# Up projection of a two-layer decoder: late weight sums pinned to their columns, their tiles taken from other rings, put-off halves in five steps, and the next layer's parameters loaded earlier

## Chip, cores and metric

The kernel runs on one core of a Trainium2 chip. The metric is the device time of one execution in microseconds. Before the change it is 1697.03 us, the median of three runs (1696.28 to 1697.89). The engines are called PE (TensorE, matrix multiply), DVE (VectorE), ACT (ScalarE), POOL (GpSimd) and SP (SyncE). Each runs its own instructions in the order in which they stand in its row of the program; SP, POOL and ACT also issue transfers (DMA).

## What is computed

Two residual layers on 512 positions of width 1024, all in float32. Each layer has a token mixer (three branches) and then a gated MLP with a causal convolution of width 3. The change lies around the MLP:

```
def conv_ffn(h, w_up, conv_w, conv_b, w_down):
    S = h.shape[1]
    u = h @ w_up
    up = jnp.pad(u, ((0, 0), (CONV_WIDTH - 1, 0), (0, 0)))
    c = conv_b
    for j in range(CONV_WIDTH):
        c = c + conv_w[j] * up[:, j:j + S]
    gate, val = jnp.split(c, 2, axis=-1)
    return (jax.nn.silu(gate) * val) @ w_down
...
    for l in range(DEPTH):
...
        x = x + conv_ffn(rmsnorm(x, norm2_g[l]), ffn_w_up[l], ffn_conv_w[l], ffn_conv_b[l], ffn_w_down[l])
    return rmsnorm(x, final_g)
```

Here w_up is 1024 x 5632 and w_down is 2816 x 1024 for each layer.

## The kernel before

**Products in three passes.** A float32 product is made of three faster ones: each operand is split into a high part and a rest. For a weight tile of 128 x 512 (a unit), `load` (L124) brings the raw tile `wr` by an SP transfer, `part` (L164) makes the high part by a copy on ACT (L175, `sh` or `wh`) and the rest by a subtraction on DVE (L178, `sl` or `wl`), and `mm3` (L190, L194) issues the three matmuls. `unit` (L97) runs loading and splitting some units ahead of their use, by a plan that a first pass over the program has recorded.

**Up projection, `ffn_up` (L1169).** 44 columns in pairs i = 0 to 21, the gate column and then the value column. For each column `colF` makes 24 matmuls on two units. Then DVE scales the result (`fu`, L1197), ACT makes the first tap of the convolution (`cv`, L1199), and DVE the other two (L1200, L1201). After a pair comes the gated product `fth` (L1206 on ACT, L1207 on DVE). Two pairs make a piece for the down projection, which works on 2 x 2 blocks with fewer products than the plain form: `halves` (L1217) prepares sums and differences of two products `fth`, for the last piece as `hs` and `hd`. It is a generator, called on in steps; the steps of the last piece are put off into the down projection, where `tail4` (L1250) takes one at each of its calls n = 3, 4, 5 and 6. Parts of the pieces are also written to memory (`ab` and `s4`, on POOL) and loaded again later.

**Late sums, `presum` (L283).** The down projection also needs sums of four blocks of w_down. `PRE` (L27) lists which are made in the up projection: nine groups in layer 0, starting at columns 4, 8, ..., 36, and five in layer 1, at 4, 12, 20, 28 and 36. A group loads one tile `pre` in each of four columns (SP), makes one sum in each of the next four (`sum4`, L162, on DVE), and each sum is written to memory (`ts`) by POOL (`store4`, L303), one column later than its place in the code. The down projection loads it again as a weight. Groups in `NOW` (L29) are loaded and summed in the down projection of layer 1 itself (tiles `now`).

**Tiles.** Ring u has 31 tiles, ring r 16, pool f 39. A sum tile comes from f when its group starts before column 20, otherwise from u in layer 1 and from r in layer 0. Weight parts of the up projection come from these rings too; a new tile waits until the old one in its place has been read for the last time. Which place it gets is decided by the scheduler that builds the program.

**Order.** A scheduler puts the instructions of each engine into a row by priority, which is the order of the code with some parts raised. `kept` (L119) pins an instruction to its place among the pinned ones, as long as `self.keep` is set, which holds in the up projection from i = 2 on. Before the change the loads of `pre` and the splits are pinned, the sums are not.

**Parameters.** `load_pc` (L479) loads a layer's parameter columns (`pc`, 128 x 242) on ACT's queue. For layer 1 it is called at the start of `down` (L1257); five small DVE operations (`omu`, `haw`, `hka`, `oka`, `nkk`, L573 to L581) read it.

Of the kernel before, what the change touches and what calls it, by code (L numbers as in the profile page):

```python
# [53 lines left out]
class Emit:  # L54
# [228 lines left out]
    def presum(self, l, c):  # L283

        for at, q in PRE[l].items():
            n = c - at
            if 0 <= n < 4:
                self.pre[l, q, n] = t = (self.f if at < 20 else self.u if l else self.r)(n="pre")
                self.kept(self.nc.sync.dma_start(t, self.raw4(l, q, (1, 3, 0, 2)[n])))
            if 4 <= n < 8:  # L290
                b = [self.pre[l, q, k] for k in (2, 0, 3, 1)]
                p = (7, 5, 6, 4)[n - 4]
                self.stores.append(((l, q), p, self.sum4(b, p)[0]))
            if 5 <= n < 9:
                self.store4(n=1)
# [116 lines left out]
    def run(self):  # L412
# [24 lines left out]
        for step in "z0 w z1 w z2 w z3 s0 s1 w z4 s2 z5 s3 w c z6 s4 w z7 s5 s6 s7 w w".split():  # L437
            if step == "w":
                if self.plan:
                    if self.nraw == self.npart:  # L440
                        self.load(self.plan[self.nraw])
                    self.part(self.plan[self.npart])
            elif step == "c":
                g1 = self.pc
                self.load_pc(0)
                tc.keep_in_program_order(nc.scalar.dma_start(self.con, a["con"]))
                self.pc, g1 = g1, self.pc
            elif step[0] == "z":
                self.norm_z(st, xs[int(step[1])], "n1")
            else:  # L450
                self.norm_sq(st, xs[int(step[1])])
# [27 lines left out]
    def load_pc(self, l):  # L479
        self.pc = self.sp.tile([128, NPC], F32, name=self.nm("pc"), tag="pc")  # L480
        self.tc.keep_in_program_order(self.nc.scalar.dma_start(self.pc, self.a["pcols"][l]))

# [83 lines left out]
    def rwkv(self, l, nst):  # L566
# [61 lines left out]
        def prep(m):  # L628
# [25 lines left out]
            A.activation(tha, pA, AF.Tanh, scale=0.5, bias=haw[:, m:m + 1])  # L654
            V.tensor_tensor(x[:, :, 64:128], q8(r), Ein, op=MUL)
            V.scalar_tensor_tensor(x[:, :, 0:64], q8(k), self.p("kk", m), Eex, op0=MUL, op1=MUL)
            V.scalar_tensor_tensor(kkn, tha, 1.0, k, op0=ADD, op1=MUL)
            A.activation(tha, tha, AF.Identity, scale=hka[:, m:m + 1], bias=oka[:, m:m + 1])
            V.scalar_tensor_tensor(bk[:, :, 0, :], q8(kkn), nkk[:, m:m + 1], q8(Eout), op0=MUL, op1=MUL)
            kp = k  # L660
            V.tensor_tensor(kp, k, tha, op=MUL)
            V.tensor_tensor(bk[:, :, 1, :], q8(kp), q8(Eout), op=MUL)
            f = F[:, m, 0:7]
# [505 lines left out]
    def ffn_up(self, l, st, x):  # L1169
# [10 lines left out]
        for i in range(NFF):  # L1180
# [6 lines left out]
            for j in (i, NFF + i):  # L1187
# [14 lines left out]
                cs.append(t)  # L1202
                self.presum(l, 2 * i + len(cs) - 1)
            g, v = cs
            th = self.u(n="fth")
# [11 lines left out]
    def halves(self, l, a, b, q, at):  # L1217
# [4 lines left out]
        else:  # L1222
            s, d = self.u(n="hs"), self.u(n="hd")
        ab = self.dp.tile([128, 512], F32, name=self.nm("ab"))
# [11 lines left out]
        V.tensor_tensor(s[:, h[0]], a[:, h[1]], b[:, h[1]], op=ADD)  # L1236
        V.tensor_tensor(s[:, h[1]], s[:, h[0]], a[:, h[0]], op=SUB)
        V.tensor_tensor(d[:, h[0]], b[:, h[0]], s[:, h[1]], op=SUB)
        P.dma_start(self.s4[:, h[q % 2]], d[:, h[0]])
# [10 lines left out]
    def tail4(self, act, n):  # L1250

        if 2 < n < 7:
            next(self.tail, None)
# [3 lines left out]
    def down(self, act, x, st):  # L1257


        nc, V, A, P, po = self.nc, self.nc.vector, self.nc.scalar, self.nc.gpsimd, self.tc.keep_in_program_order  # L1260
        self.load_pc(1)
        Q, H, N = NFF // 2, [slice(0, 256), slice(256, 512)], {}
# [450 lines left out]
```

## Time and profile before

One execution was profiled. Its own time is 1696.14 us, its span in the trace 1694.4 us, its mean granted clock 0.998.

| | |
|---|---|
| median of three runs | 1697.03 us |
| profiled execution, its own time | 1696.14 us |
| its span | 1694.4 us |
| ACT busy | 819.1 us (48%) |
| POOL busy | 295.2 us (17%) |
| HBM read and written | 233.25 MB and 56.89 MB |

Stages, in us from the start of the span: mixer of layer 0 up to about 500, its up projection to 738, its down projection to 867, mixer of layer 1 to 1345, its up projection to 1583, its down projection (`last`) to the end.

A row of the timeline gives start, length, engine, line of the kernel, operation, and output and inputs by the program's names without numbers; in brackets stands how long the engine was idle before, and for what. A row of a group gives busy time, the mean of one instruction in ns, and the idle time of its engine just before. A row of waits gives total, number and longest.

### The profile page before, as it was taken

The numbers are of one execution on the slowest core, as the hardware profiler recorded it, in microseconds if no ns is written. First come the engines' busy times: TensorE is split into PE (matmuls) and PEld (weight loads), VectorE is DVE, ScalarE is ACT, GpSimd is POOL, SyncE is SP. The second block draws the span as 40 slices with busy tenths as digits, with TensorE's granted clock in tenths as the row PEclk, the third lists the DMA queues.
The fourth block names the chain that finished last, engine by engine and source line by source line (L and its number), as shares of the span: only waits on it lengthen the run. The fifth ranks groups of instructions, "written<-read, shape, count | busy, mean of one in ns | idle before, by whom it ended". The sixth has DMA issues, their size and how long they took to land.

```text
span 1694.4 us, 29267 instructions
## 1 busy us (share of the span) xinstructions
PE 1677.2 (99%) x10643; PEld 1393.3 (82%) x10643; DVE 1290.5 (76%) x2289; ACT 819.1 (48%) x1436; POOL 295.2 (17%) x438
## 2 busy tenths in 40 slices
PE   9999999999999999999999999999999999999998
PEld 7888877888888887789988887778888888888787
DVE  7887746578578988887868877565785688888886
ACT  6563533554254444456655634335543444444565
POOL 1121013312200111100111210223132022221000
PEclk9999999999999999999999999999999999999999
DMA  5236565634434665667733365646344445555865
GB/s 182 90 110 210 183 201 162 187 119 137 162 115 152 216 209 191 202 222 262 232 112 95 106 202 178 210 154 193 121 141 144 155 162 182 192 186 171 283 193 173
DMA packets 155904, 292.09 MB, mean 172 GB/s; under 512 B 21552, under 2 KB 32560, under 8 KB 155760
## 3 DMA queue, kind: packets, MB, share of 16 engines
q1 hardware_dynamic: 127136, 213.97, 39.9%
q0 software_dynamic: 20272, 61.10, 10.6%
q10 hardware_dynamic: 8352, 15.15, 2.5%
q8 instruction: 83, 1.36, 0.3%
q14 instruction: 61, 0.50, 0.1%
HBM read 233.25 MB, written 56.89 MB: 171 GB/s over the span
## 4 chain that ended last, share of the span: by engine, by line
PE 71%; issue 16%; DVE 5%; DMA 4%; POOL 2%; ACT 1%; SPq 0%; ACTq 0%; DVEq 0%; POOLq 0%
PE acc L194 60%; PE sm L194 5%; PE sm L766 2%; DMA pre<-wdt 2%; DMA wr<-wall 1%; PE sm L1022 1%; DVE sl L178 1%; POOL ts L303 1%; PE sm L673 1%; DVE wl L178 1%; POOL gth L1145 1%; PE sm L1133 0%; DVE pre L162 0%; DVE cv L1201 0%; DMA wr<-ts 0%
## 5 line engine op out<-in xcount | busy, mean ns | idle before, releaser
L194 PE MATMUL acc<-lo,sh 128*128 128x512 f32 (+1 forms) x1144 | 442.9, 387 | 1.3 <-ACT sh L175 1.3
L194 PE MATMUL acc<-hi,sh 128*128 128x512 f32 (+1 forms) x1144 | 441.7, 386 | 0.0
L194 PE MATMUL acc<-hi,sl 128*128 128x512 f32 (+1 forms) x1144 | 431.4, 387 | 2.3 <-DVE sl L178 2.3
L175 ACT CAST sh<-wr 128x512 fp32r<-128x512 f32 x350 | 210.8, 615 | 198.5 <-PE acc L194 105.0
L178 DVE TENSOR_TENSOR wl<-wr,wh 128x512 fp32r<-128x512 f32 x276 | 193.9, 706 | 139.6 <-ACT wh L175 132.3
L175 ACT CAST wh<-wr 128x512 fp32r<-128x512 f32 x276 | 169.5, 619 | 265.3 <-PE acc L194 184.0
L178 DVE TENSOR_TENSOR sl<-wr,sh 128x512 fp32r<-128x512 f32 x350 | 239.2, 692 | 71.1 <-ACT sh L175 62.7
L194 PEld LDWEIGHTS acc<-hi,sl 128*128 128x128 f32 x1144 | 214.9, 188 | 49.6 <-DVE sl L178 6.3
L194 PEld LDWEIGHTS acc<-lo,sh 128*128 128x128 f32 x1144 | 214.9, 188 | 45.7 <-ACT sh L175 2.1
L194 PEld LDWEIGHTS acc<-hi,sh 128*128 128x128 f32 x1144 | 214.9, 188 | 42.8
L194 PE MATMUL acc<-lo,wh 128*128 128x512 f32 (+1 forms) x636 | 244.8, 385 | 0.0
L194 PE MATMUL acc<-hi,wl 128*128 128x512 f32 (+1 forms) x636 | 243.0, 382 | 0.0
L194 PE MATMUL acc<-hi,wh 128*128 128x512 f32 (+1 forms) x636 | 242.4, 381 | 0.0
L1199 ACT ACTIVATE cv<-fu,pc 128x512 f32<-128x512 f32 x88 | 71.7, 816 | 179.6 <-DVE fu L1197 179.5
L194 PEld LDWEIGHTS acc<-hi,wl 128*128 128x128 f32 x636 | 119.6, 188 | 24.8 <-DVE wl L178 1.1
L194 PEld LDWEIGHTS acc<-lo,wh 128*128 128x128 f32 x636 | 119.6, 188 | 23.4 <-ACT wh L175 0.2
L194 PEld LDWEIGHTS acc<-hi,wh 128*128 128x128 f32 x636 | 119.6, 188 | 22.4 <-issue 0.2
L194 PE MATMUL acc<-wl,hi 128*128 128x512 f32 x212 | 85.7, 404 | 0.0
L1200 DVE SCALAR_TENSOR_TENSOR cv<-fu,pc,cv 128x511 f32<-128x511 f32 x88 | 65.8, 748 | 22.5 <-ACT cv L1199 22.3
L194 PE MATMUL acc<-wh,lo 128*128 128x512 f32 x212 | 82.5, 389 | 0.0
L194 PE MATMUL acc<-wh,hi 128*128 128x512 f32 x212 | 82.4, 389 | 0.0
L1201 DVE SCALAR_TENSOR_TENSOR cv<-fu,pc,cv 128x510 f32<-128x510 f32 x88 | 65.7, 747 | 1.7
(422 smaller groups left out, 2601.7 us busy)
## 6 DMA issues: line engine op xcount, KB each, us to landing
wr<-wall SPq DMA_DIRECT2D x480, 256.0 KB, 3.0
wr<-ts SPq DMA_DIRECT2D x72, 256.0 KB, 4.0
wr<-wdt SPq DMA_DIRECT2D x66, 256.0 KB, 3.5
pre<-wdt SPq DMA_DIRECT2D x56, 256.0 KB, 3.6
ts<-pre POOLq DMA_DIRECT2D x56, 256.0 KB, 2.9
gd<-gth ACTq DMA_DIRECT2D x48, 256.0 KB, 2.8
gth<-gd POOLq DMA_DIRECT2D x48, 256.0 KB, 3.6
sp<-ab SPq DMA_DIRECT2D x22, 256.0 KB, 4.9
```

The costliest lines, as they stand in the source:

```text
L175: self.kept(self.nc.scalar.copy(hi[:, :n], raw[:, :n]))
L178: self.kept(self.nc.vector.tensor_tensor(lo[:, :n], raw[:, :n], hi[:, :n], op=SUB))
L194: i = self.nc.tensor.matmul(*x, **y, **kw)
L303: po(self.nc.gpsimd.dma_start(self.tsum[*q, p], t))
L673: i = T.matmul(pK[hv[1 - h], j, :], bk[hv[h], c, 1, :], x[hv[h], c, :], start=True, stop=True)
L766: po(T.matmul(o, l, r, start=start, stop=True, skip_group_check=True))
L1022: po(T.matmul(o, lhsT, rhs, start=start, stop=stop, skip_group_check=True))
L1145: nc.gpsimd.dma_start(t, self.gd[br, m])
L1199: A.activation(t, u, AF.Identity, scale=self.p("cw2", j), bias=self.p("cb", j))
L1200: V.scalar_tensor_tensor(t[:, 1:], u[:, :511], self.p("cw1", j), t[:, 1:], op0=MUL, op1=ADD)
L1201: V.scalar_tensor_tensor(t[:, 2:], u[:, :510], self.p("cw0", j), t[:, 2:], op0=MUL, op1=ADD)
```

## The change

1. The late sums are pinned (`kept`), and each is stored in the column in which it is made.
2. Their tiles: in layer 0 groups that start before column 24 use pool f, those at 24 and 32 ring u, those at 28 and 36 ring r; in layer 1 all use ring u.
3. The last piece's `hs` and `hd` come from ring r in place of u. Its preparation has one more step, and `tail4` takes the five steps at n = 3, 5, 7, 9 and 11.
4. The parameters of layer 1 are loaded in the up projection of layer 0 after pair 16, and `down` only switches to them.
5. In the mixer, seven instructions for block 0 are raised in priority.

```diff
@@ presum
-                self.pre[l, q, n] = t = (self.f if at < 20 else self.u if l else self.r)(n="pre")
+                self.pre[l, q, n] = t = (self.u if l or at in (24, 32) else self.f if at < 24 else self.r)(n="pre")
...
-                self.stores.append(((l, q), p, self.sum4(b, p)[0]))
-            if 5 <= n < 9:
+                t, i = self.sum4(b, p)
+                self.kept(i)
+                self.stores.append(((l, q), p, t))
                 self.store4(n=1)
@@ run
-                self.load_pc(0)
+                self.pc = self.load_pc(0)
@@ load_pc
-        self.pc = self.sp.tile([128, NPC], F32, name=self.nm("pc"), tag="pc")
-        self.tc.keep_in_program_order(self.nc.scalar.dma_start(self.pc, self.a["pcols"][l]))
+        pc = self.sp.tile([128, NPC], F32, name=self.nm("pc"), tag="pc")
+        self.tc.keep_in_program_order(self.nc.scalar.dma_start(pc, self.a["pcols"][l]))
+        return pc
@@ rwkv, prep
+            with self.tc.high_priority() if m == 0 else nullcontext():
+                V.tensor_tensor(x[:, :, 64:128], q8(r), Ein, op=MUL)
...
@@ ffn_up
+            if i == 16 and not l:
+                self.npc = self.load_pc(1)
@@ halves
-            s, d = self.u(n="hs"), self.u(n="hd")
+            s, d = self.r(n="hs"), self.r(n="hd")
...
         V.tensor_tensor(s[:, h[1]], s[:, h[0]], a[:, h[0]], op=SUB)
+        yield
         V.tensor_tensor(d[:, h[0]], b[:, h[0]], s[:, h[1]], op=SUB)
@@ tail4
-        if 2 < n < 7:
+        if 2 < n < 13 and n % 2:
             next(self.tail, None)
@@ down
-        self.load_pc(1)
+        self.pc = self.npc
```

In the rows below each instruction is given by its line, operation, output and inputs with their numbers (the last number counts all tensors), and its size. Numbers and lines differ a little between the two programs.

**First place: DVE in layer 0, columns 6 and 7 of the up projection.** sl_1205 is the rest of a weight unit that PE reads later; pre_1200 is a late sum tile. Before:

```order
L162 TENSOR_TENSOR pre_1190_5791<-pre_1190_5791,pre_1179_5743 128x512
L178 TENSOR_TENSOR sl_1197_5815<-wr_1185_5767,sh_1196_5814 128x512
L1197 TENSOR_TENSOR fu_1198_5830<-acc_1191_5793,rsF_1125_5509 128x512
L1234 TENSOR_TENSOR ah_1213_5882<-fth_1180_5745,ah_1212_5881 128x256
L162 TENSOR_TENSOR pre_1200_5836<-pre_1200_5836,pre_1190_5791 128x512
L1200 SCALAR_TENSOR_TENSOR cv_1199_5832<-fu_1198_5830,pc_41_176,cv_1199_5832 128x511
L1201 SCALAR_TENSOR_TENSOR cv_1199_5832<-fu_1198_5830,pc_41_176,cv_1199_5832 128x510
L1207 SCALAR_TENSOR_TENSOR fth_1201_5838<-fth_1201_5838,cv_1199_5832 128x512
L178 TENSOR_TENSOR sl_1205_5845<-wr_1192_5794,sh_1204_5844 128x512
```

And now:

```order
L178 TENSOR_TENSOR sl_1197_5815<-wr_1185_5767,sh_1196_5814 128x512
L1200 TENSOR_TENSOR fu_1198_5830<-acc_1191_5793,rsF_1125_5509 128x512
L1239 TENSOR_TENSOR ah_1213_5882<-fth_1180_5745,ah_1212_5881 128x256
L1203 SCALAR_TENSOR_TENSOR cv_1199_5832<-fu_1198_5830,pc_41_176,cv_1199_5832 128x511
L1204 SCALAR_TENSOR_TENSOR cv_1199_5832<-fu_1198_5830,pc_41_176,cv_1199_5832 128x510
L1212 SCALAR_TENSOR_TENSOR fth_1201_5838<-fth_1201_5838,cv_1199_5832 128x512
L178 TENSOR_TENSOR sl_1205_5845<-wr_1192_5794,sh_1204_5844 128x512
```

The sums have left these columns. Over the whole up projection of layer 0 there is now one sum in each column from 8 to 43, right behind the column's second cv; before, the first four stood in columns 5 to 7, and the last in column 39.

**Second place: DVE at the end of layer 0's up projection.** sl_1699 is the rest of a weight unit of the down projection; omu to nkk are the small operations on the parameters. Before:

```order
L1200 SCALAR_TENSOR_TENSOR cv_1681_7790<-fu_1680_7788,pc_41_176,cv_1681_7790 128x511
L1201 SCALAR_TENSOR_TENSOR cv_1681_7790<-fu_1680_7788,pc_41_176,cv_1681_7790 128x510
L178 TENSOR_TENSOR sl_1699_7818<-wr_1661_7700,sh_1698_7817 128x512
L573 TENSOR_SCALAR omu_2026_9461<-pc_1685_7802 128x14
L575 TENSOR_SCALAR haw_2027_9463<-pc_1685_7802 128x8
L577 TENSOR_SCALAR hka_2028_9465<-pc_1685_7802 128x4
L178 TENSOR_TENSOR wl_1708_7872<-wr_1674_7752,wh_1707_7871 128x512
L579 TENSOR_SCALAR oka_2029_9467<-pc_1685_7802 128x4
L581 TENSOR_SCALAR nkk_2030_9469<-pc_1685_7802 128x4
L1207 SCALAR_TENSOR_TENSOR fth_1683_7797<-fth_1683_7797,cv_1681_7790 128x512
```

And now:

```order
L1203 SCALAR_TENSOR_TENSOR cv_1683_7794<-fu_1682_7792,pc_41_176,cv_1683_7794 128x511
L1204 SCALAR_TENSOR_TENSOR cv_1683_7794<-fu_1682_7792,pc_41_176,cv_1683_7794 128x510
L162 TENSOR_TENSOR pre_1629_7578<-pre_1629_7578,pre_1618_7530 128x512
L178 TENSOR_TENSOR sl_1699_7818<-wr_1663_7704,sh_1698_7817 128x512
L178 TENSOR_TENSOR wl_1708_7872<-wr_1676_7756,wh_1707_7871 128x512
L1212 SCALAR_TENSOR_TENSOR fth_1685_7801<-fth_1685_7801,cv_1683_7794 128x512
```

The five small operations have moved some ten columns up. The last sum, pre_1629, has come down to a place between the last cv and sl_1699.

**Third place: DVE at the end of layer 1's up projection.** now_3681 is a sum of the down projection, sl_3692 the rest of one of its weight units, hs, hd and ah the put-off halves. Before:

```order
L1236 TENSOR_TENSOR hs_3684_17107<-fth_3630_16939,fth_3654_17040 128x256
L162 TENSOR_TENSOR now_3681_17098<-now_3681_17098,now_3679_17096 128x512
L1237 TENSOR_TENSOR hs_3684_17107<-hs_3684_17107,fth_3630_16939 128x256
L178 TENSOR_TENSOR wl_3697_17153<-wr_3671_17069,wh_3696_17152 128x512
L1238 TENSOR_TENSOR hd_3685_17108<-fth_3654_17040,hs_3684_17107 128x256
L178 TENSOR_TENSOR wl_3702_17169<-wr_3675_17083,wh_3701_17168 128x512
L162 TENSOR_TENSOR now_3679_17096<-now_3679_17096,now_3678_17095 128x512
L1240 TENSOR_TENSOR fth_3654_17040<-fth_3630_16939 128x256
L187 TENSOR_TENSOR ah_3694_17141<-hs_3684_17107,ah_3693_17140 128x512
L178 TENSOR_TENSOR sl_3692_17137<-wr_3668_17057,sh_3691_17136 128x512
```

And now:

```order
L1241 TENSOR_TENSOR hs_3684_17107<-fth_3631_16941,fth_3655_17042 128x256
L178 TENSOR_TENSOR sl_3690_17122<-wr_3649_17015,sh_3689_17121 128x512
L1242 TENSOR_TENSOR hs_3684_17107<-hs_3684_17107,fth_3631_16941 128x256
L162 TENSOR_TENSOR now_3681_17098<-now_3681_17098,now_3679_17096 128x512
L178 TENSOR_TENSOR sl_3692_17132<-wr_3668_17057,sh_3691_17131 128x512
L1244 TENSOR_TENSOR hd_3685_17108<-fth_3655_17042,hs_3684_17107 128x256
L178 TENSOR_TENSOR wl_3695_17146<-wr_3671_17069,wh_3694_17145 128x512
```

sl_3692 now follows directly on the sum now_3681; before, seven operations stood between them. On SP the order is the same in both programs, and so it is on PE but for ten pairs of neighbouring matmuls.

More of the change, by code (lines that the diff above doesn't have):

```diff
@@ L654, in prep @@
             A.activation(tha, pA, AF.Tanh, scale=0.5, bias=haw[:, m:m + 1])
[L655 to L662, printed above, removed]
+            with self.tc.high_priority() if m == 0 else nullcontext():
+                V.tensor_tensor(x[:, :, 64:128], q8(r), Ein, op=MUL)
+                V.scalar_tensor_tensor(x[:, :, 0:64], q8(k), self.p("kk", m), Eex, op0=MUL, op1=MUL)
+                V.scalar_tensor_tensor(kkn, tha, 1.0, k, op0=ADD, op1=MUL)
+                A.activation(tha, tha, AF.Identity, scale=hka[:, m:m + 1], bias=oka[:, m:m + 1])
+                V.scalar_tensor_tensor(bk[:, :, 0, :], q8(kkn), nkk[:, m:m + 1], q8(Eout), op0=MUL, op1=MUL)
+                kp = k
+                V.tensor_tensor(kp, k, tha, op=MUL)
+                V.tensor_tensor(bk[:, :, 1, :], q8(kp), q8(Eout), op=MUL)
             f = F[:, m, 0:7]
```

## The prediction

> **What bounds the kernel now.** I read the page's busy times first, then the table by stretches, then the waits of TensorE (PE), and last the timeline around its longest waits.
>
> ```profile
> span 1694.4 us, 29267 instructions
> ...
> PE 1677.2 (99%) x10643; PEld 1393.3 (82%) x10643; DVE 1290.5 (76%) x2289; ACT 819.1 (48%) x1436; POOL 295.2 (17%) x438
> ```
>
> PE is busy 99% of the span, so a change that takes no matmul away can only win what PE loses between matmuls. "Busy" hides part of that, because matmuls overlap in the pipe. Counting them over equal stretches is better (length, busy time and count of each engine, granted clock, DMA share, GB/s):
>
> ```profile
> 500.00:738.00 238.00, 234.47 (x1023) 190.80 (x1022) 204.32 (x343) 107.85 (x182) 30.25 (x56) 1.00 0.58 191
> ...
> 1345.00:1583.00 238.00, 237.91 (x1050) 196.69 (x1049) 203.07 (x331) 108.54 (x177) 49.17 (x90) 1.00 0.54 176
> 1583.00:1623.00 40.00, 36.94 (x158) 30.14 (x157) 32.99 (x57) 21.21 (x37) 2.16 (x4) 0.96 0.93 310
> ```
>
> These are the up projection of layer 0, that of layer 1, and the start of the last down projection. Layer 1 fits 1050 matmuls into 238 us, 0.2267 us each, almost without idleness. Layer 0 fits 27 fewer into the same 238 us: 27 x 0.2267 = **6.1 us lost**. The last stretch holds 158, where 40 / 0.2267 would be 176; about **4 us are lost** there. So what the edits can win lies in two places, 10 to 11 us or 0.6% of the span. The waits in and behind the first stretch (500 to 750 us: total, times, longest) are all for the second or the first half of a weight split:
>
> ```profile
> PE acc L194 <- DVE sl L178: 2.8, 5, 0.7
> PE acc L194 <- ACT sh L175: 1.3, 2, 0.9
> ```
>
> **Layer 0, sums pinned one to a column.** Within 500 to 738 us, the sums and what they wait for (busy, mean ns | idle before, releaser):
>
> ```profile
> L175 ACT CAST sh<-wr 128x512 fp32r<-128x512 f32 x82 | 49.0, 612 | 26.3 <-PE acc L194 13.4 <-DMA ts<-pre 6.5 <-DMA wr<-wall 4.0
> ...
> L162 DVE TENSOR_TENSOR pre<-pre,pre 128x512 f32<-128x512 f32 x36 | 24.8, 690 | 17.4 <-DMA pre<-wdt 16.5 <-PE acc L194 0.4
> ```
>
> VectorE (DVE) stood still 16.5 us with a sum at the head of its row whose tile had not landed. One such wait, from sum to matmul:
>
> ```profile
> 542.37 0.69 DVE L162 TENSOR_TENSOR pre<-pre,pre 128x512 f32<-128x512 f32 x1 [2.42 <-DMA pre<-wdt]
> ...
> 544.63 0.39 PE L194 MATMUL acc<-lo,sh 128*128 128x512 f32 x1
> 544.85 0.39 PE L194 MATMUL acc<-hi,sh 128*128 128x512 f32 x1
> ...
> 545.23 0.68 DVE L178 TENSOR_TENSOR sl<-wr,sh 128x512 fp32r<-128x512 f32 x1
> 545.97 0.50 PE L194 MATMUL acc<-hi,sl 128*128 128x512 f32 x1 [0.73 <-DVE sl L178]
> ```
>
> DVE loses 2.42 us, the weight split sl behind it comes late, and PE starts 1.12 us after the matmul before, in place of 0.23: 0.89 us. The second kind goes through ScalarE (ACT):
>
> ```profile
> 654.91 0.62 ACT L175 CAST sh<-wr 128x512 fp32r<-128x512 f32 x1 [3.14 <-DMA ts<-pre]
> ...
> 655.58 0.50 PE L194 MATMUL acc<-lo,sh 128*128 128x512 f32 x1 [0.86 <-ACT sh L175]
> ```
>
> Here the weight's new tile in ring r was a sum's, whose store landed at 654.9; that cost PE 1.0 us (0.86 recorded, and the 0.16 that the pipe hid above, 0.89 - 0.73). Transfers take (KB each, median us from issue to landing):
>
> ```profile
> pre<-wdt SPq DMA_DIRECT2D x56, 256.0 KB, 3.6
> ts<-pre POOLq DMA_DIRECT2D x56, 256.0 KB, 2.9
> ...
> now<-wdt SPq DMA_DIRECT2D x16, 256.0 KB, 5.5
> ```
>
> A pinned sum reads tiles that were asked for three columns earlier or more; a column is 24 x 0.2267 = 5.4 us, and 3.6 fit into one. So the DVE waits go, and with them the first kind of stall. The sums stay 36, so DVE's work does not grow. The second kind shrinks, since fewer sum tiles live in ring r: in the new order three casts (columns 34, 35, 36) still take a tile that the sum of the column before has just left. I price them at 0.5 us together. The bounds are 0 (the sum sits early in its column, and 2.9 us of landing fit into the rest) and 3 x 1.0 = 3.1 us by the row at 655.58; I stay near 0, because there the sum itself was late, which it no longer is. Term: -6.1 + 0.5 = **-5.6 us**, bounds -6.1 and -3.0.
>
> **End of layer 0, parameters and one more sum.**
>
> ```profile
> 743.59 0.75 DVE L1201 SCALAR_TENSOR_TENSOR cv<-fu,pc,cv 128x510 f32<-128x510 f32 x1
> 744.25 0.69 DVE L178 TENSOR_TENSOR sl<-wr,sh 128x512 fp32r<-128x512 f32 x1
> 745.75 0.17 DVE L573 TENSOR_SCALAR omu<-pc 128x14 f32<-128x14 f32 x1 [0.81 <-DMA pc<-pcols]
> ```
>
> ```profile
> 745.00 0.39 PE L194 MATMUL acc<-ah,sl 128*128 128x256 f32 x1 [0.52 <-DVE sl L178]
> ...
> 752.66 0.39 PE L194 MATMUL acc<-ah,sl 128*128 128x256 f32 x1 [0.22 <-DVE sl L178]
> ```
>
> The early load takes the 0.81 us wait and five small operations out of DVE here. What is late at 745.00, however, is sl_1699, and it stands ahead of them, so this stall doesn't profit. It grows: the last sum of layer 0 is now pinned between cv and sl_1699, and each such DVE operation sets the next back by 0.6 us (744.25 after 743.59 shows the step). I take +0.6 (bounds 0, if DVE reaches the column earlier, and 0.7). The stall at 752.66 goes, since sl_1720 now stands ahead of the halves' work and DVE arrives 0.8 us earlier: -0.5, with the part the pipe hides (bounds -0.5 and 0). Together **+0.1 us**. The load itself and the five operations in column 33 cost nothing: DVE has 34 us free in those 238. Without that cover they would cost at most 5 x 0.17 = 0.9 us.
>
> **Layer 1, inside the up projection.** There is nothing to win, as 1050 matmuls fit. The 20 late tiles now all come from ring u and are held some columns longer, so a few conv tiles (columns 50, 53, 56) reuse tiles whose store is recent. I followed those stores: they are issued two or more columns earlier, against a landing of 2.9 us. The halves' five steps leave the copy back over fth close behind its store; DVE waits for such landings by tenths already:
>
> ```profile
> 1411.36 0.42 DVE L1240 TENSOR_TENSOR fth<-fth 128x256 f32<-128x256 f32 x1 [0.22 <-DMA ab<-fth]
> ```
>
> I take **+0.3 us** (one to two such waits reaching PE), bounds 0 and 4 (four columns of 1.0 us, as at 655.58).
>
> **End of layer 1.** This is the largest single stall:
>
> ```profile
> 1584.86 0.42 DVE L1236 TENSOR_TENSOR hs<-fth,fth 128x256 f32<-128x256 f32 x1
> 1588.12 0.69 DVE L162 TENSOR_TENSOR now<-now,now 128x512 f32<-128x512 f32 x1 [2.84 <-DMA now<-wdt]
> 1588.73 0.42 DVE L1237 TENSOR_TENSOR hs<-hs,fth 128x256 f32<-128x256 f32 x1
> ...
> 1592.14 0.68 DVE L178 TENSOR_TENSOR sl<-wr,sh 128x512 fp32r<-128x512 f32 x1
> ```
>
> ```profile
> 1589.21 0.61 PE L194 MATMUL acc<-sh,ah 128*128 128x512 f32 x2
> 1592.88 0.79 PE L194 MATMUL acc<-sl,ah 128*128 128x512 f32 x1 [3.06 <-DVE sl L178]
> 1593.47 1.05 PE L194 MATMUL acc<-sh,ah 128*128 128x512 f32 x2
> 1594.32 0.63 PE L194 MATMUL acc<-sl,ah 128*128 128x512 f32 x1
> ...
> 1596.00 0.62 PE L194 MATMUL sm<-wh,ah 128*128 128x512 f32 x2
> ```
>
> ```profile
> 1589.60:1592.90 3.30, 0.24 (x2) 0.02 (x1) 3.30 (x8) 2.90 (x6) 1.62 (x3) 0.95 1.06 388
> 1592.90:1596.00 3.10, 3.10 (x7) 2.46 (x8) 3.10 (x6) 1.14 (x2) 0.00 (x0) 0.51 0.95 217
> ```
>
> PE wanted sl_3692 at 1589.21 + 2 x 0.227 = 1589.66 and started at 1592.88: 3.2 us. Then seven starts take 3.12 us (1592.88 to 1596.00) in place of 1.59, at a granted clock of 0.51: 1.5 us more, 4.7 in all. The weight had long landed. DVE first waited 2.84 us for the tile of a "now" sum, and then did seven other operations before sl_3692. In the new order sl_3692 stands directly behind that sum, and its cast directly behind sh_3689 on ACT. With the landing unchanged it starts at 1588.73 and ends at 1589.4, in time. Behind it come ten DVE operations (eight full ones, two halves of 0.34) before sl_3706, which then ends 6.1 us after sl_3692; PE wants it 24 matmuls, 5.4 us, after. So 0.4 to 0.7 us of waiting appear there. If the stores of the last two sums, which now fall into columns 42 and 43, push the landing back by one transfer of 0.7 us (256 KB at the 388 GB/s of the row at 1589.60), sl_3692 is 0.4 us late as well. I take 1.0 us left: **-3.7 us**, bounds -4.3 and 0.
>
> [...]
>
> **The rest.** The other rings, hs and hd in r and the raised priority of the mixer's rows change no order on an engine that waits: 0. The sum is -5.6 + 0.1 + 0.3 - 3.7 = **-8.9 us**. The profiled execution took 1696.14 us, so 1687.2; the median of before is 0.89 above it, so **1688.1 us**.
>
> **Rivals.** (1) *The "now" tiles land later.* The DMA share of 1.06 in the row at 1589.60 speaks for it: the engines are full. If the landing slips by 3 us, sl_3692 ends at 1592.4, 2.7 us late, the slow stretch returns with its 1.5 us, and 0.7 wait at sl_3706: 4.9 lost in place of 4.7, and the sum is -5.6 + 0.1 + 0.3 + 0.2 = -5.0: **1692.0**. Against it: only two transfers of 0.7 us are new nearby. [...] (2) *DVE is crowded, not blocked.* It is busy 204 of 238 us in layer 0; sums at fixed places could sit ahead of an sl that PE needs next, as at sl_1699. Half of the 6.1 us would stay: **1690.6**. Against it: layer 1 has the same 203 us and loses nothing. (3) *The change does not do what it says:* sums are made two to three columns later and free their tiles later, so the casts' waits for stores (6.5 us of ACT in before) multiply. Eight sums live in r; at 1.0 us each the gain is gone: **1696**. Against it: only three casts follow a store closely. (4) *Slower:* ring u starves in layer 1. All 20 late tiles sit in its 31 tiles beside the norm's; if a column's cv waits for a store, its fu, cv and sl all shift. It decides from 0.6 us lost for each of the 20 sums, 12.3 us = 8.9 + 3.4; at 0.8 us each, **1704**. Against it: those stores are columns old.
>
> **How the numbers follow.** Forecast (1685 to 1690) 0.58; rival 1 0.16; rival 2 0.13; rival 3 0.08; rival 4 0.05. 0.2% of 1697.03 is 3.4 us, about what a measurement can tell from no change. Faster than that (below 1693.6) are the forecast, rival 2 and most of rival 1: 0.84; within it rival 3 and the rest of 1: 0.11; slower rival 4: 0.05. The range goes from all terms at their good bounds (-6.1 - 0.5 + 0 - 4.3 = -10.9, and 0.75 for the spread of the runs: 1685.4, taken as 1685.0) to rival 1 with the three casts at their bad bound (1692.0 + 2.6, taken as 1695.0).
>
> **What would show it.** Right: 500 to 738 us holds near 1048 matmuls; DVE's idle time before sums of "pre" falls from 16.5 us to under 2; PE's 3.06 us wait and the stretch at clock 0.51 are gone; a wait of 1 us or more stands near 745. Wrong: ACT casts waiting for "ts" stores in layer 0, conv rows waiting for "ab" or "ts" stores in layer 1, or a "now" sum that starts after 1589.5 by the old clock.

## The result and the profile after

The changed kernel takes **1692.61 us** (median of ten runs, 1690.04 to 1693.72); the kernel before took 1697.09 us on the same chip (ten runs). The ratio is 0.9975, 95% interval 0.9965 to 0.9985: 4.5 us faster, where 8.9 us were forecast. The profiled execution took 1690.48 us.

The page of the changed kernel gives the span and the busy times. They show little, as before: PE's busy time fell by 1.2 us, less than one per mille.

```profile
span 1688.8 us, 29263 instructions
...
PE 1676.0 (99%) x10643; PEld 1394.4 (83%) x10643; DVE 1288.3 (76%) x2289; ACT 820.0 (49%) x1436; POOL 295.0 (17%) x438
```

The table by stretches answers to the three rows that carried the prediction. It is here with 22 us behind the first stretch beside it (length, busy time and count of PE, weight loads, DVE, ACT, POOL, granted clock, DMA share, GB/s).

```profile
500.00:738.00 238.00, 236.07 (x1036) 194.33 (x1035) 204.85 (x350) 109.85 (x184) 29.15 (x55) 0.99 0.58 192
738.00:760.00 22.00, 20.98 (x175) 20.78 (x175) 16.72 (x29) 12.05 (x22) 2.12 (x4) 1.00 0.75 235
1345.00:1583.00 238.00, 238.00 (x1050) 196.51 (x1049) 204.34 (x333) 107.71 (x176) 49.38 (x92) 1.00 0.54 176
1583.00:1623.00 40.00, 39.64 (x174) 32.19 (x173) 35.19 (x60) 22.93 (x40) 1.52 (x3) 1.00 0.95 339
```

The last down projection came out as forecast: 174 matmuls in place of 158, and the clock is back at 1.00. Layer 1 stayed full. Layer 0 gained 13 matmuls and not 25: the clock of 0.99 is a first sign that something in it is now slow that was not before. The groups of ACT and DVE in this stretch show that it is not DVE waiting at the sums:

```profile
L175 ACT CAST sh<-wr 128x512 fp32r<-128x512 f32 x83 | 50.3, 614 | 45.2 <-PE acc L194 19.3 <-DMA wr<-wall 14.5 <-issue 9.2
...
L162 DVE TENSOR_TENSOR pre<-pre,pre 128x512 f32<-128x512 f32 x35 | 24.0, 686 | 0.0
```

DVE's 16.5 us of idleness in front of sums are gone. But ACT now waits 19.3 us for PE in front of casts, where it was 13.4 us before. Its 6.5 us for the stores of sums have become one wait (waits of ACT, 500 to 765 us):

```profile
ACT sh L175 <- DMA ts<-pre: 1.4, 1, 1.4
```

For a balance by stages I took each distance from the start of one matmul to the start of the next, less the commonest distance of its shape, and added these up. This counts a slow clock and the waits that the pipe hides as well. (A stretch without any loss comes out at -0.3 us, by rounding; it is shown as 0. With the -0.3 counted, the gain in the last column is 5.6 us, which is what the two profiled spans differ by.)

| us lost between matmuls | 500-722 (layer 0, interior) | 722-765 (end of layer 0) | 1335-1572 (layer 1, interior) | 1572-1612 (end of layer 1) | all four |
|---|---|---|---|---|---|
| before | 6.2 | 1.2 | 0 | 4.7 | 12.1 |
| after | 0 | **5.8** | 0 | 1.4 | 7.2 |

By the table the gain is 12.1 - 7.2 = 4.9 us in these stages. Nearly all that is missing sits between 722 and 741 us, where before lost nothing. The timeline of DVE there, in the changed kernel (start, length, row, idle before):

```profile
724.14 0.69 DVE L178 TENSOR_TENSOR sl<-wr,sh 128x512 fp32r<-128x512 f32 x1 [1.44 <-issue]
727.32 0.69 DVE L178 TENSOR_TENSOR sl<-wr,sh 128x512 fp32r<-128x512 f32 x1 [2.48 <-PE acc L194]
727.93 0.68 DVE L1200 TENSOR_TENSOR fu<-acc,rsF 128x512 f32<-128x512 f32 x1
...
730.95 0.69 DVE L162 TENSOR_TENSOR pre<-pre,pre 128x512 f32<-128x512 f32 x1
731.55 0.69 DVE L1212 SCALAR_TENSOR_TENSOR fth<-fth,cv 128x512 f32<-128x512 f32 x1
732.15 0.69 DVE L178 TENSOR_TENSOR sl<-wr,sh 128x512 fp32r<-128x512 f32 x1
```

And PE, with the table by stretches around it:

```profile
728.06 0.50 PE L194 MATMUL acc<-hi,sl 128*128 128x512 f32 x1 [0.16 <-DVE sl L178]
...
730.88 0.40 PE L194 MATMUL acc<-hi,sh 128*128 128x512 f32 x1
732.89 0.50 PE L194 MATMUL acc<-hi,sl 128*128 128x512 f32 x1 [1.61 <-DVE sl L178]
...
734.08 0.63 PE L194 MATMUL acc<-lo,sh 128*128 128x512 f32 x1
```

```profile
732.80:736.60 3.80, 3.71 (x10) 2.94 (x11) 3.21 (x7) 1.84 (x3) 0.00 (x0) 0.62 0.84 268
```

DVE stands still 1.44 and 2.48 us with a split (sl_1654, sl_1657) at the head of its row. The weight is there; what is missing is the tile for the result. The program's order says why: the old tile in that place of ring r is a weight half that PE reads until 4 matmuls (0.9 us) before it wants the new one. For sl_1654, sl_1657 and sl_1665 this distance is 4 matmuls in the new order; in the old one it is 26 or more. The trace names PE for the second wait; for the first it names nothing ("issue"), but in both cases DVE starts 0.1 us after the end of the matmul that stands 4 before the one that wants the split. By the places that the program gives the tiles, ring r with its 16 holds eight tiles xi (the layer's input, kept for the down projection), four of the last group (start 36, held until its sums in columns 40 to 43 are stored) and one ah of the down projection. Three places are left, and a weight unit needs two. The fu, cv, sum and fth behind the second wait start late, so sl_1665 is done at 732.84, and PE starts 1.78 us late. Then the clock falls to 0.62. Together 4.6 us: delays of 0.43, 0.43, 0.19 and 1.78, and 1.7 for the slow stretch.

The end of layer 1, DVE and PE in the changed kernel:

```profile
1586.65 0.69 DVE L162 TENSOR_TENSOR now<-now,now 128x512 f32<-128x512 f32 x1 [2.71 <-DMA now<-wdt]
1587.26 0.68 DVE L178 TENSOR_TENSOR sl<-wr,sh 128x512 fp32r<-128x512 f32 x1
...
1593.35 0.69 DVE L178 TENSOR_TENSOR sl<-now,sh 128x512 fp32r<-128x512 f32 x1
```

```profile
1588.00 0.50 PE L194 MATMUL acc<-sl,ah 128*128 128x512 f32 x1
...
1594.09 0.50 PE L194 MATMUL acc<-sl,ah 128*128 128x512 f32 x1 [0.36 <-DVE sl L178]
```

DVE still waits 2.71 us for the "now" tile, but sl_3692 stands right behind that sum and is out at 1587.94; PE starts on it at 1588.00, 0.13 us late.

### The profile page after: what moved, and what is told of

Read it like the earlier page. It is cut to its first block, busy times and chain, and to the rows that moved or that the text cites. A ratio compares the mean times of both kernels' runs of the same rounds, so it can differ in the third digit from the quotient of the medians.

```text
span 1688.8 us, 29263 instructions
## 1 busy us (share of the span) xinstructions
PE 1676.0 (99%) x10643; PEld 1394.4 (83%) x10643; DVE 1288.3 (76%) x2289; ACT 820.0 (49%) x1436; POOL 295.0 (17%) x438
## 4 chain that ended last, share of the span: by engine, by line
PE 93%; DVE 3%; issue 2%; DMA 1%; ACT 1%; POOL 0%; ACTq 0%; SPq 0%; DVEq 0%; POOLq 0%
PE acc L194 82%; PE sm L194 5%; PE sm L769 2%; PE sm L1025 1%; DVE wl L178 1%; PE sm L676 1%; DMA wr<-wall 1%; PE sm L1136 0%; DMA now<-wdt 0%; DVE TMP L897 0%; PE acc L423 0%; DVE sl L178 0%; ACT wh L175 0%; DVE cs L899 0%; DMA tr<-bkT 0%
## 5 line engine op out<-in xcount | busy, mean ns | idle before, releaser
L1200 DVE TENSOR_TENSOR fu<-acc,rsF 128x512 f32<-128x512 f32 x88 | 60.3, 686 | 14.5 <-PE acc L194 14.2
```

What stands on the lines that cost most here:

```text
L1200: V.tensor_tensor(u, ps, self.rsF, op=MUL)
```

## The experiments

"Tile theory" in the expectations is the reading above: splits wait in ring r for tiles that PE has only just read. Its rival, "crowding", is that the pinned sums fill DVE's row. All ratios are to the kernel before on the same chip. The losses are those of one profiled execution, in the stages of the table above; the two mixers lost 52 to 58 us in these executions (52.4 before, 52.4 after; 61 in one, named below), so spans and times alone don't rank these kernels within some 5 us. DVE's order in the mixers is the same before and after, by the names in the trace, so the raised priority, the only edit there, changed nothing in it.

**The changed kernel again, unaltered.**

> The changed kernel once more, unaltered. In its first profile PE lost 4.5 us between 722 and 738 us (starts late by 0.3, 0.3 and 1.8 us, then eight matmuls 0.43 us apart), 1.3 us at 744 and 1.4 us around 1577 to 1595; span 1688.8 us. Its ten times lie in two groups, four at 1690.0 to 1690.8 and six at 1692.6 to 1693.7. If the stalls are fixed by the order and the tiles (both theories), they stand at the same places again, within 0.3 us each, whichever group this execution falls into. If a time of the upper group has some 2 us more at 722 to 738, that place is unstable, and part of the missing gain is its spread.

1692.71 us, ratio 0.9973 (0.9964 to 0.9983). The loss in 722-765 us was 5.8 us again, at the same splits. The stall belongs to the program's order, not to one execution.

**The last group of layer 0 in ring u.**

```
-                self.pre[l, q, n] = t = (self.u if l or at in (24, 32) else self.f if at < 24 else self.r)(n="pre")
+                self.pre[l, q, n] = t = (self.u if l or at in (24, 32, 36) else self.f if at < 24 else self.r)(n="pre")
```

> The changed kernel with the tiles of layer 0's last group (start at column 36) from ring u in place of ring r. Tile theory: with these four tiles in r until column 43, the splits sl_1654, sl_1657 and sl_1665 get tiles that PE reads until four matmuls (0.9 us) before it wants the new ones; so DVE waits for PE, and PE then for DVE. With the group in u the nearest such distance in columns 36 to 41 is 26 matmuls (5.9 us): the 4.5 us between 722 and 738 vanish (under 0.5), the stall at 744 stays at 1.2, span 1684.4 us, time about 4.4 us under the changed kernel, ratio to before 0.9949. Crowding theory (three sums pinned in columns 41 to 43 are too much for DVE beside the first splits of the down projection): the sums are as many, so 4 us stay and the time is that of the changed kernel within 0.5 us.

1690.06 us, ratio 0.9956 (0.9941 to 0.9971). The sums stand where they stood in DVE's row, to within one place (three splits near columns 38 to 40 have moved up by a few), yet 722-741 us lost 0.5 us in place of 4.6. The time is 2.7 us below the unaltered run on the same chip, where 4.4 were expected; in its profiled execution the mixers lost 56.9 us, against 54.9 in that run. Run once more, beside a later experiment:

> The changed kernel with the last group of layer 0's sums in ring u once more, to stand beside the run with earlier last groups on one chip. Tile theory: loss between matmuls of 0.5 us in 722-741, 1.3 in 741-765, 1.1 in 1572-1612, none in the interiors, and 2 to 4 us less time than the changed kernel (1692.6), whatever the mixers do. If the gain of the first run was chance: 722-741 lies near 4.6 us again, and the time is 1692 to 1693.

1688.29 us, ratio 0.9948 (0.9932 to 0.9964); 0.5 us again. The table by stretches of this second run:

```profile
500.00:738.00 238.00, 238.00 (x1070) 197.92 (x1068) 208.01 (x356) 111.93 (x188) 29.64 (x55) 1.00 0.59 195
```

PE is never idle in layer 0 up to 738 us. Crowding has fallen as the cause of the 4.6 us: DVE is busier here (208.0 us) than in the changed kernel (204.9), and PE waits less.

**One tile more in ring r, one fewer in ring u**, with the rings of the change.

```
-NU, NR, NFP = 31, 16, 39
+NU, NR, NFP = 30, 17, 39
```

> The changed kernel with one tile more in ring r (17) and one fewer in ring u (30); the sums stand in the same rows and rings. Tile theory (the splits of columns 40 and 41 wait for tiles that PE reads until 4 matmuls before their first use): with one tile more this distance is 15 matmuls, 3.4 us, so the loss in 722-741 us falls from 4.57 us to 0-1.0; what 30 tiles do to ring u is unknown, 0 to 2 us in layer 1's interior. Rival (DVE is crowded there by the pinned sums): the same sums stand in the same places, so 4 to 5 us stay lost in 722-741. Time 1688.5 to 1691 by the first, 1692 to 1693 by the second.

A half hit. 722-741 us lost 0.8 us, as the tile theory wants (the distance for the three splits is now 15 matmuls). But the time was a miss: 1697.80 us, ratio 1.0004 (0.9991 to 1.0017). The loss moved to 743-749 us, where it was 3.9 us. DVE, ACT and PE:

```profile
728.68 0.69 DVE L178 TENSOR_TENSOR sl<-wr,sh 128x512 fp32r<-128x512 f32 x1 [1.55 <-ACT sh L175]
```

```profile
728.02 0.62 ACT L175 CAST sh<-wr 128x512 fp32r<-128x512 f32 x1 [2.05 <-PE acc L194]
```

```profile
745.55 0.58 PE L194 MATMUL acc<-ah,sl 128*128 128x256 f32 x1 [1.43 <-DVE sl L178]
```

The casts have the same problem as the splits: ACT waited 2.05 us for PE, DVE 1.55 us for that cast, and this lateness came out at the crowded place behind column 43. One tile doesn't free the ring. Besides, the mixers lost 61 us here. The order of some loads and of some DVE operations there has changed with the ring sizes; whether that is the cause wasn't tried.

**The halves' five steps alone** (hs and hd in r, the second `yield`, steps at n = 3, 5, ..., 11), in the kernel before.

```
-            s, d = self.u(n="hs"), self.u(n="hd")
+            s, d = self.r(n="hs"), self.r(n="hd")
...
+        yield
...
-        if 2 < n < 7:
+        if 2 < n < 13 and n % 2:
```

> The kernel before with the third edit alone: hs and hd from ring r, one more step, steps at n = 3, 5, 7, 9, 11; sums, tiles and parameters as before. If the steps' spacing is what puts sl_3692 behind its sum, the 4.7 us at the end of layer 1 fall to 1.0 to 1.4, layer 0 keeps its 6.1 us: span 1690.9 us, 3.4 less than before, ratio 0.998. If it is the pinned sums (or their later stores) that change the order or the landing there, the 4.7 us stay and the time is that of before.

1695.78 us, ratio 0.9987 (0.9973 to 1.0002). In the profile the end of layer 1 lost nothing, against 4.7 us before and 1.4 us after:

```profile
1583.00:1623.00 40.00, 40.00 (x178) 33.14 (x177) 37.25 (x62) 24.73 (x44) 2.16 (x4) 1.00 0.93 327
```

The interior of layer 0 lost 5.0 us and its end 0.8. So the steps alone win the whole of the last place, and the rest of the change gives 1.1 to 1.5 us of it back. This is read from the stage: the interval of the time includes no change, and the mixers lost 5 us more in this execution than in that of before.

**The pins alone**, in the kernel before.

```
-                self.stores.append(((l, q), p, self.sum4(b, p)[0]))
-            if 5 <= n < 9:
+                t, i = self.sum4(b, p)
+                self.kept(i)
+                self.stores.append(((l, q), p, t))
                 self.store4(n=1)
```

> The kernel before with the first edit alone: sums pinned and stored in their column, tiles from the rings of before (layer 0's last five groups all in r). Tile theory: in columns 25 to 41 some twenty splits now get a tile that PE reads until 3 to 6 matmuls before it wants the new one, in four groups like the one that cost 4.5 us in the changed kernel, and one in each column between; the old 6.1 us go and 15 to 25 us come, so the time is 9 to 19 us above before, ratio 1.005 to 1.011. Crowding theory: one sum to a column is harmless except at the end; the time is 1.5 us below before (-6.1 + 4.5), ratio 0.999.

1707.49 us, ratio 1.0056 (1.0038 to 1.0074): 9.6 us slower than before, at the lower edge of what the tile theory gave, and crowding failed. 500-722 us lost 9.9 us, 722-765 lost 7.0, and the end of layer 1 kept its 4.9. Groups within 500 to 738 us, and what PE waits for in 500 to 765:

```profile
L175 ACT CAST sh<-wr 128x512 fp32r<-128x512 f32 x82 | 49.9, 617 | 57.4 <-PE acc L194 40.1 <-DMA wr<-wall 7.2 <-issue 6.5
...
L162 DVE TENSOR_TENSOR pre<-pre,pre 128x512 f32<-128x512 f32 x33 | 22.6, 685 | 0.0
```

```profile
PE acc L194 <- DVE sl L178: 5.1, 14, 1.6
PE acc L194 <- ACT sh L175: 1.9, 7, 0.4
```

The pins do take away all of DVE's idleness at sums (0.0), and PE loses more for it. A pinned sum holds its four tiles three or four columns longer, and casts wait 40.1 us for PE (13.4 before). The loss has two parts: up to 638 us the pins alone lose nothing, where before lost 0.9 us; from 638 to 722 us, with the sums' tiles in ring r, they lose 10.1 us, where before lost 5.2.

**The rings alone**, in the kernel before.

```
-                self.pre[l, q, n] = t = (self.f if at < 20 else self.u if l else self.r)(n="pre")
+                self.pre[l, q, n] = t = (self.u if l or at in (24, 32) else self.f if at < 24 else self.r)(n="pre")
```

> The kernel of before with the changed rings of the late tiles alone: sums not pinned, four at once, old steps, old parameter load. Theory (the pins win the interior of layer 0, the rings only make room for them): DVE still idles 10 us or more in front of sums whose tile has not landed, the loss between matmuls in 500-722 us stays at 4 to 7 us (6.2 before), 722-765 loses 1 to 2 us, 1572-1612 the 4.7 of before; the time lies within 2 us of before. Rival (the rings alone win the interior, because fewer casts wait for the stores of sums in ring r): 500-722 loses 2 us or less, and the time is 4 us or more below before.

("Four at once" is inexact: unpinned, the four sums of a group fall into three columns, soon after their loads, such as 25, 26, 27 and 27.) My theory fell, and the rival held for the loss; the time is 3.5 us below before, short of its 4. 500-722 us lost 0.5 us and 722-765 0.7, with DVE still idle 12.1 us at sums (17.4 before):

```profile
500.00:738.00 238.00, 237.59 (x1066) 197.04 (x1065) 207.38 (x351) 111.25 (x188) 30.24 (x56) 1.00 0.59 196
```

```profile
L162 DVE TENSOR_TENSOR pre<-pre,pre 128x512 f32<-128x512 f32 x36 | 24.8, 688 | 12.1 <-DMA pre<-wdt 11.8
```

1691.01 us, ratio 0.9974 (0.9961 to 0.9987). By the balance (4.3 us lost in the four stages) 7.8 us should have been won, and 3.5 were; the run of the steps alone falls short in the same way (6.2 and 2.1). In that run the mixers lost 5 us more than before; here they did not in the profiled execution (52.6), which was also among the quickest of its runs. What the others lost wasn't profiled. The 2.8 us at the end of layer 1 are one delay of 2.67 us with no slow stretch behind it, where before has 3.22 and 1.5 for the stretch.

After this run I split the row of before on which the first term rested at 638 us; from there on the sums' tiles come from ring r (groups from 20 on). Before, 500-638 us and then 638-722 us:

```profile
L175 ACT CAST sh<-wr 128x512 fp32r<-128x512 f32 x49 | 29.2, 612 | 16.8 <-PE acc L194 11.3 <-DMA wr<-wall 3.1 <-issue 1.8
...
L162 DVE TENSOR_TENSOR pre<-pre,pre 128x512 f32<-128x512 f32 x20 | 13.8, 689 | 8.3 <-DMA pre<-wdt 8.2
```

```profile
L175 ACT CAST sh<-wr 128x512 fp32r<-128x512 f32 x29 | 17.3, 612 | 9.5 <-DMA ts<-pre 6.5 <-PE acc L194 2.1 <-DMA wr<-wall 0.9
...
L162 DVE TENSOR_TENSOR pre<-pre,pre 128x512 f32<-128x512 f32 x15 | 10.4, 691 | 9.0 <-DMA pre<-wdt 8.3 <-PE acc L194 0.4
```

The rings alone, 638-722 us:

```profile
L175 ACT CAST sh<-wr 128x512 fp32r<-128x512 f32 x30 | 18.0, 612 | 8.9 <-PE acc L194 3.8 <-issue 3.1 <-DMA wr<-wall 2.0
...
L162 DVE TENSOR_TENSOR pre<-pre,pre 128x512 f32<-128x512 f32 x16 | 11.0, 688 | 4.9 <-DMA pre<-wdt 4.6
```

In before DVE idles as much in the first part (8.2 us) as in the second (8.3 us). But PE loses 0.9 us in the first and 5.2 us in the second, where alone casts wait for the stores of sums. Those casts are not all of it: of the 5.2 us some 2.1 stand behind them (at 655.58 and 662.45), and some 2.3 behind splits that followed a sum for whose tile DVE had waited (at 674.92, 714.08 and 720.05). With the rings alone no cast waits for a store in this part, DVE still waits 4.6 us for tiles, once for 1.81 us, and PE loses nothing. So the rings decide, and the same kind of DVE wait does harm or none. By which step ring r took the splits' lead away in before wasn't tried.

**The changed kernel without its pins.**

```
-                t, i = self.sum4(b, p)
-                self.kept(i)
-                self.stores.append(((l, q), p, t))
+                self.stores.append(((l, q), p, self.sum4(b, p)[0]))
+            if 5 <= n < 9:
                 self.store4(n=1)
```

> The changed kernel without its pins: sums free and four at once as in before, with the new rings, the new steps and the early parameters. Theory (the rings win the interior of layer 0 and the steps the end of layer 1; the pins only cost): loss between matmuls 0.5 to 1 us in 500-722 with DVE still idle 8 us or more in front of sums, 0.5 to 1.3 in 722-765 (5.84 in the changed kernel), 0 to 0.4 in 1572-1612 (1.35 in the changed kernel), so 5 to 6 us less lost in these stages than in the changed kernel; ratio 0.992 to 0.996. Rival (with the steps the free sums fall in front of the splits at the layer ends): 3 us or more lost in 722-765 or 1572-1612, ratio 0.997 or more.

1687.71 us, ratio 0.9950 (0.9932 to 0.9969). 500-722 us lost 1.1 us, 722-765 lost 0.6, the end of layer 1 nothing; 1.7 in all against 7.2 in the changed kernel. The two stretches:

```profile
500.00:738.00 238.00, 237.45 (x1061) 196.10 (x1060) 206.97 (x355) 110.71 (x187) 30.23 (x56) 1.00 0.59 196
```

```profile
1583.00:1623.00 40.00, 40.00 (x178) 33.14 (x177) 37.07 (x61) 24.23 (x43) 0.00 (x0) 1.00 0.89 319
```

**The parameters loaded at the old place, without the raised priority**, in the changed kernel.

```
-            with self.tc.high_priority() if m == 0 else nullcontext():
+            with nullcontext():
...
-            if i == 16 and not l:
-                self.npc = self.load_pc(1)
...
-        self.pc = self.npc
+        self.load_pc(1)
```

> The changed kernel with the parameters of the next layer loaded where before loads them, and without the raised priority. Theory (the 0.81 us wait for the parameters stood behind the split that PE wanted, so it cost nothing): the wait is back on DVE near 745, the loss in 741-765 us stays at 1.2 to 1.4, and the time is that of the changed kernel within 0.5 us. Rival (the early load is what took the stall at 752.66 away, since DVE arrived 0.8 us earlier): that stall is back with 0.3 to 0.5 us, and 741-765 loses 1.6 to 1.8 us.

1692.78 us, ratio 0.9982 (0.9971 to 0.9994). DVE near the end of layer 0, and PE:

```profile
742.64 0.68 DVE L178 TENSOR_TENSOR sl<-wr,sh 128x512 fp32r<-128x512 f32 x1
744.20 0.17 DVE L574 TENSOR_SCALAR omu<-pc 128x14 f32<-128x14 f32 x1 [0.88 <-DMA pc<-pcols]
```

```profile
743.38 0.39 PE L194 MATMUL acc<-ah,sl 128*128 128x256 f32 x1 [1.47 <-DVE sl L178]
```

The wait is back with 0.88 us, behind the split that PE wants, and PE loses nothing after it: the early load is worth no measurable time here. My number for 741-765 was off (2.2 us in place of 1.2 to 1.4), because PE arrived earlier: in this execution no slow stretch followed the stall at 732.9. DVE sets the start at sl_1699, so of the 1.6 us saved before it 0.9 were spent there again.

**The last groups earlier**, with that of layer 0 in ring u.

```
-PRE = {0: {4 + 4 * k: 2 + k for k in range(9)}, 1: {4: 0, 12: 1, 20: 2, 28: 4, 36: 6}}
+PRE = {0: {4 + 4 * k - (k == 8): 2 + k for k in range(9)}, 1: {4: 0, 12: 1, 20: 2, 28: 4, 34: 6}}
...
-                self.pre[l, q, n] = t = (self.u if l or at in (24, 32) else self.f if at < 24 else self.r)(n="pre")
+                self.pre[l, q, n] = t = (self.u if l or at in (24, 32, 35) else self.f if at < 24 else self.r)(n="pre")
```

> The changed kernel with the last group of layer 0's sums in ring u, and with the last groups one column earlier in layer 0 (35 in place of 36) and two earlier in layer 1 (34 in place of 36), so that no sum stands in column 43 of layer 0 nor in columns 42 and 43 of layer 1. Theory (what is left at the two layer ends comes from the last pinned sums, which stand ahead of the splits that PE wants next): the loss between matmuls in 741-765 us falls from 1.3 us to 0.7-0.9 (as with the halves' steps alone, 0.78), and in 1572-1612 us from 1.1-1.35 us to 0-0.3; 722-741 stays at 0.5 or less; the time is 1.4 to 1.6 us below that of the run with the last group in u alone, 1687.5 to 1689. Rival (two groups that overlap in a column put two loads of 256 KB and two sums side by side and cost that column a stall): a new loss of 0.5 to 2 us within 500-741 us or 1335-1572 us, and no gain over that run.

1686.03 us, ratio 0.9934 (0.9917 to 0.9950). 722-765 us lost 1.2 us in place of 1.8 (one DVE step of 0.6 us less ahead of sl_1699; it falls into 739-741 us here, so the split at 741 in the expectation cut it off), the end of layer 1 0.3. On the same chip the run with the last group in u alone took 1688.29 us, 2.3 us more. Once more, on another chip:

> The kernel with the last groups earlier and that of layer 0 in ring u once more, to see whether its gain holds on another chip: by the loss between matmuls (about 1.2 us in 722-765, 0.3 in 1572-1612, none in the interiors) 10 to 11 us less than before, ratio 0.992 to 0.995. If the first run owed part of its time to the mixers: 0.995 to 0.997.

1686.84 us, ratio 0.9955 (0.9939 to 0.9971), with 1.2 us lost in the four stages. The loss came as expected, but the time is 7.6 us below before and not 10 to 11: the ratio lies in the second band of the expectation, and its interval reaches into both. Why the time falls short of the loss stays open, as in the runs of the rings and of the steps alone. All that PE waited for splits in 500 to 765 us:

```profile
PE acc L194 <- DVE sl L178: 0.4, 1, 0.4
PE acc L194 <- ACT sh L175: 0.2, 1, 0.2
```

| kernel | 500-722 | 722-765 | 1335-1572 | 1572-1612 | all four | median us | ratio |
|---|---|---|---|---|---|---|---|
| pins alone | 9.9 | 7.0 | 0 | 4.9 | 21.8 | 1707.5 | 1.0056 |
| steps alone | 5.0 | 0.8 | 0.1 | 0 | 5.9 | 1695.8 | 0.9987 |
| rings alone | 0.5 | 0.7 | 0.4 | 2.8 | 4.3 | 1691.0 | 0.9974 |
| the change | 0 | 5.8 | 0 | 1.4 | 7.2 | 1692.6 | 0.9975 |
| the change, one tile more in r | 0 | 4.7 | 0 | 0.7 | 5.5 | 1697.8 | 1.0004 |
| the change, old parameter load | 0 | 5.2 | 0 | 0.9 | 6.1 | 1692.8 | 0.9982 |
| the change without pins | 1.1 | 0.6 | 0 | 0 | 1.7 | 1687.7 | 0.9950 |
| the change, last group in u | 0 | 1.8 | 0 | 1.1 | 2.9 | 1690.1 | 0.9956 |
| the same, last groups earlier | 0 | 1.2 | 0 | 0.3 | 1.5 | 1686.0 | 0.9934 |

The last row and the one without pins beat the kernel before by 0.4 to 0.7%. Their losses (1.5 and 1.7 us) also lie well below the change's 7.2; the times say so less surely, since the intervals of the run without pins and of the change just meet and the two ran on different chips. Which of the two is better stays open.

## Why the prediction was wrong

The direction was right, and the size half. By its own steps:

- **Interior of layer 0, -5.6 us.** The size held (6.2 lost before, nothing after), and DVE's idleness went as foretold. But the reason failed, so the size came right by luck. The prediction put the gain down mainly to the pins ("the DVE waits go, and with them the first kind of stall"); the rings had a part in the second kind ("fewer sum tiles live in ring r") and 0 under the rest. The runs show the reverse: the rings alone take this loss from 6.2 to 0.5 us, and the pins alone raise it to 9.9. The pins' reason holds for about 1 us: up to 638 us they alone take 0.9 us to nothing, and on top of the rings they take the last 0.5 to 1.1 us. Of DVE's 16.5 us in front of sums some 3.3 us reached PE.
- **End of layer 0, +0.1 us.** The stall at sl_1699 came as reckoned: a delay of 1.17 us at 744.03 against 0.68 before, and that at 752.66 went. That the parameters cost nothing was right too. What the sum lacked is **the missing term, +4.6 us at columns 40 to 42**. The step that failed: in the part on pinned sums I followed only tiles that are freed by a sum's store ("fewer sum tiles live in ring r"; three casts, 0.5 us), and not the weight halves that share the ring and are freed by PE. With the input's eight tiles, four of the sums and an ah in a ring of 16, three places are left, and a new half is split only when PE has all but used up an old one. -8.9 + 4.6 = -4.3, and -4.5 was measured.
- **Layer 1, interior, +0.3 us.** Nothing was lost; inside its bounds.
- **End of layer 1, -3.7 us.** Measured -3.4 (4.7 to 1.35; 1.1 in the second execution; 1.5 of the 4.7 was the slow stretch), by the mechanism foretold. The wait at the later split was 0.52 us, inside the 0.4 to 0.7. The steps do this alone; the pins take the rest back.
- **Rivals.** The "now" sum came 1.47 us earlier than before and PE wanted its split 1.79 us earlier (1587.87, after 1589.66), so the landing slipped 0.3 us against PE and not 3 (rival 1). Crowding (2) is refuted for the 4.6 us by the run with the last group in u; at the two layer ends the last pinned sums do cost 0.6 and about 1 us, as the run with earlier groups shows. Rival 3 came nearest: ring r did starve, but through tiles that PE holds; for a store ACT waited once, 1.4 us. Ring u did not starve (4).
- **The signs.** Three of four came: no idleness before sums, the 3.06 us wait and its slow stretch gone, a wait of 1 us near 745. The count of 1048 was the fourth; 1036 stood there. The count was a poor sign: the run that loses nothing there holds 1070, because half-size matmuls of the down projection, 0.12 us apart, then fall into the stretch.

## What to carry to other kernels

Fixing an instruction to a later place lengthens the life of every tile that it reads. Count in the program's order, for each tile of each ring, how many matmuls lie between the last reader of the old content and the first use of the new one: four here cost 4.6 us, 15 moved the loss to a later place, 26 cost nothing. And before an idle time is taken for a cause, split its row by stretches: the same 8 us of idle DVE went with 1 us of lost PE time in one part and with 5 in the next, so the idle time alone didn't decide.

## What the runs showed of the hardware that was not expected

The clock fell after a wait half as long as the one that I had in view (1.61 us, against 3.06 in before). After it the changed kernel took 0.39 to 0.43 us for each of seven matmuls (the row at 732.80 above, clock 0.62). The run with the old parameter load has the same wait at the same place and no such stretch:

```profile
732.90 0.50 PE L194 MATMUL acc<-hi,sl 128*128 128x512 f32 x1 [1.61 <-DVE sl L178]
...
732.80:736.60 3.80, 3.70 (x22) 3.30 (x22) 3.21 (x7) 1.84 (x3) 0.00 (x0) 1.00 0.81 259
```

In the up projections and at their ends, over all profiles here, delays of 1.6 to 1.8 us were followed by a slow stretch four times out of six, two of 2.7 and 3.2 us both times, one of 2.67 us (the rings alone) not, and those up to 1.3 us never. The stretch costs 1.4 to 1.7 us each time. It also doesn't always start with the first matmul after the wait: in the changed kernel that came at 732.89 and the slow ones from 734.08 on.

The granted clock in these traces is 1.00 or 0.50. Each of the six slow stretches in the stages above lasts 3.41 us (1592.54 to 1595.95 in before). That of the changed kernel, with the 3.42 us ahead of it:

```profile
730.31:733.73 3.42, 1.81 (x8) 1.01 (x7) 3.42 (x6) 1.63 (x4) 0.54 (x1) 1.00 0.33 125
733.73:737.14 3.41, 3.41 (x11) 2.73 (x10) 2.82 (x6) 1.84 (x3) 0.00 (x0) 0.50 0.89 282
```

PE was busy 1.81 us of the 3.42 ahead of the fall. What decides whether a slow stretch follows was not shown: the wait of 1.61 us was followed by one in the changed kernel and by none in the run with the old parameter load. So the 1.7 us behind such a wait can come in one execution and stay out in another, and the 1.5 us of the slow stretch in before's 4.7 may be absent in other executions of it.
